# A hybrid attention and retention trunk on one core: the front's hand-written order, decay tables, retention norm and batch 1's x

## The chip, the cores and the metric

The kernel runs on 1 core of one Trainium2 chip. A core has five engines that run beside each other, each with its own instruction stream: TensorE (PE, matmuls; PEld is its weight load), VectorE (DVE), ScalarE (ACT), GpSimd (POOL) and SyncE (SP, which here issues most DMAs). They wait for each other through semaphores. The metric is the device time of one execution in microseconds, the median over runs.

## The reference

Two sequences ("prompt" and "sample", called batch 0 and batch 1 below) of 512 positions with 1024 features pass through one layer, in float32:

```python
mod = silu(c) @ w_ada + b_ada                       # adaLN, six sections of 1024
sh1, sc1, g1, sh2, sc2, g2 = split(mod, 6)
h = rms_norm(x, norm1_g) * (1.0 + sc1) + sh1
proj = h @ w_in                                     # 1024 -> 2816
q_a, k_a, v_a, q_r, k_r, v_r, g_r = split(proj)     # 512, 128, 128, 512, 512, 512, 512
o_a = windowed_attention(q_a, k_a, v_a, sink)       # 8 heads, |t - s| <= 128, ALiBi
o_r = bidirectional_retention(q_r, k_r, v_r, g_r, decay_fwd, decay_bwd)   # 4 heads
x = x + g1 * (concat(o_a, o_r) @ w_out)
h = rms_norm(x, norm2_g) * (1.0 + sc2) + sh2
x = x + g2 * (square(relu(h @ w_mlp1)) @ w_mlp2)    # 1024 -> 4096 -> 1024
return rms_norm(x, final_g)
```

Retention of a head weighs the score of positions t and s by exp(|t - s| * log g), with one decay forward and one backward, and normalizes each row of its result over the head's 128 features: `(y - mean) * rsqrt(var + eps)`, then multiplies by `silu(g_r)`.

## The kernel before

Every product of two matrices is made in three passes of a rounded format: a value is split into a high part (a cast on ACT: `wh`, `hh`) and a low part (value minus high part, on DVE: `wl`, `hl`), and `mm3` (L117) multiplies high by high, high by low and low by high. A weight unit is 128 x 1024 and is loaded, cast and subtracted (`split_unit`, L95) before PE can use it; batch 0 writes both parts back to DRAM (`kept_first`, `kept_rv`, `kept_in`), and batch 1 loads them from there (`kept_unit`, L108).

The program runs in stages. The **front** computes batch 0's RMS norm, the first two adaLN sections for batch 0 and the first six column units of w_in (768 columns: attention's Q, K and V), which are accumulated in six PSUM banks named `first`. Its order is written out by hand in `FRONT` (L1093): a string of steps, issued one after the other, and pinned per engine by `pin` (L1116) up to the first step of P.7. A step's number is a chunk of 128 of the 1024 features (kc, 0 to 7) or a part of it:

- `x`, `nat`, `tr`, `wi` load x, adaLN weights in two layouts, and w_in; `pm`, `mr`, `pt`, `md` make adaLN of a chunk on PE for both batches (from `nat`); `C.kc.1` and `C.kc.0` make it for batch 0 by a reduction on DVE (from `tr`; L170, the tile `jka_f`) for scale and shift.
- `xn` scales x by the norm's factors (L275); `hh` (ACT, L278), `hm` (ACT, L281) and `hl` (DVE, L284) make h's high part, h itself and its low part; `wh` (ACT, L1050) and `wl` (DVE, L1055, the tile `wil`) do the same for w_in.
- `P.kc.c` is one `mm3` of chunk kc and column unit c; 18 matmuls for each kc. `keep.kc` stores both parts of w_in's chunk (`kept_first`) through POOL's DMA queue (L1077). `lg` are the small steps of the decays' logarithms, `cbc` copies of adaLN's input from PSUM.

When P.7 of a column unit is done, its K, V or Q is cast (`ks`, `vt_a`, `qs`: L299 to L329). Then `run_units` goes through the **units** of batch 0: `pj_rv` (retention's V, four units of two), `pj_rq`, `pj_rk`, `pj_rg` of each head, while stages (attention blocks, retention heads), background jobs (adaLN of the other sections, `raw_adat_s` and `raw_adat_g`) and extra jobs are issued between a unit's matmuls. What is issued behind the front is ordered by the framework's scheduler. `norm_x1` (L1118), batch 1's RMS norm, is an extra job that a hook starts behind unit 9. The same units for batch 1 follow, then the output projection and the MLP.

A retention head (`ret_head`, L394) gets its decay table (`decay_table`, L511: an exp over 128 x 896 of distances times logarithms), and at its end takes mean and variance on DVE, the power -1/2 on POOL (`rrs`, L440), and writes four blocks `ryn` (L443) that PE transposes (`pyb`, L448).

Loads of weights go to three buffers (`raw`) or, with `spare`, to a pool of 32 (`r4f`).

## Time and profile before

| | us |
|---|---|
| median of 3 runs | 1139.08 (1136.89 to 1140.65) |
| the profiled execution | 1136.41 |
| its span | 1134.6 |
| mean granted TensorE clock | 0.991 of full speed |
| TensorE busy | 1088.0 |
| VectorE busy | 890.3 |
| ScalarE busy | 488.9 |

In the rows of the profile `A<-B xN` is an instruction that writes tile A from B, N times; a bracket `[3.79 <-DVE h]` is idle time of the engine just ahead of it, in us, with what ended it. `PEclk` is the granted clock of TensorE as a share of full speed. A matmul's own duration (some 0.39 us for 512 columns) is longer than the distance to the next, since matmuls are pipelined.

### The profile page before, as it was taken

How to read it: one execution, taken by the hardware profiler on the slowest of the kernel's cores; microseconds unless marked ns; L12 is line 12 of the kernel's file. 1: busy time of each engine (PE TensorE's matmuls, PEld its weight loads, DVE VectorE, ACT ScalarE, POOL GpSimd, SP SyncE). 2: the span in 40 equal slices, each digit the busy share in tenths (PEclk: the TensorE clock that was granted, in tenths of full speed). 3: DMA queues.
4: the chain of work that ended last, by engine and by line, in shares of the span. 5: the costliest groups of instructions: out<-in, count | busy, mean ns of one | idle time of the engine just before them, and what ended most of it. 6: DMA issues, size and time to landing. Idle time of an engine off the chain costs nothing.

```text
span 1134.6 us, 14030 instructions
## 1 busy us (share of the span) xinstructions
PE 1088.0 (96%) x4997; PEld 888.0 (78%) x4997; DVE 890.3 (78%) x1504; ACT 488.9 (43%) x827; POOL 47.2 (4%) x70
## 2 busy tenths in 40 slices
...
GB/s 374 354 212 247 223 261 322 246 216 195 190 179 162 202 303 338 322 183 23 213 220 158 161 167 177 166 155 130 232 371 103 173 189 194 213 93 185 184 21 148
DMA packets 85722, 232.73 MB, mean 205 GB/s; under 512 B 8578, under 2 KB 20882, under 8 KB 85652
## 3 DMA queue, kind: packets, MB, share of 16 engines
...
q0 software_dynamic: 1440, 6.31, 1.4%
q8 instruction: 39, 0.64, 0.2%
q10 hardware_dynamic: 288, 0.31, 0.1%
...
## 4 chain that ended last, share of the span: by engine, by line
PE 67%; DVE 9%; DMA 2%; issue 2%; ACT 2%; POOL 1%; SPq 0%; POOLq 0%; ACTq 0%; DVEq 0%
PE px_None L898 13%; PE x L1295 13%; PE py_None L898 10%; PE y L1295 10%; PE po L120 2%; PE po L121 2%; PE po L122 2%; PE po L384 1%; PE ppt L377 1%; DVE jka_s L170 1%; DVE wc_l L1235 1%; DVE x2r L1359 1%; DVE jka_g L170 1%; DMA ur<-spill 1%; DMA wl_q<-kept_first 1%
## 5 line engine op out<-in xcount | busy, mean ns | idle before, releaser
L1235 DVE TENSOR_TENSOR uc_l<-ur,uc_h 128x1024 fp32r<-128x1024 f32 x56 | 68.3, 1220 | 53.7 <-ACT uc_h L1235 36.6
L1295 PE MATMUL x<-wc_l,uc_h 128*128 128x512 f32 x256 | 99.8, 390 | 0.8 <-DVE wc_l L1235 0.8
L1295 PE MATMUL x<-wc_h,uc_h 128*128 128x512 f32 x256 | 99.4, 389 | 0.5 <-DVE u L916 0.5
L1295 PE MATMUL x<-wc_h,uc_l 128*128 128x512 f32 x256 | 99.6, 389 | 0.0
L1235 ACT CAST uc_h<-ur 128x1024 fp32r<-128x1024 f32 x56 | 58.9, 1052 | 73.8 <-PE x L1295 30.8
L1295 PE MATMUL y<-wc_h,uc_h 128*128 128x512 f32 x192 | 74.7, 389 | 0.0
L1295 PE MATMUL y<-wc_l,uc_h 128*128 128x512 f32 x192 | 74.7, 389 | 0.0
L1295 PE MATMUL y<-wc_h,uc_l 128*128 128x512 f32 x192 | 74.7, 389 | 0.0
L1235 ACT CAST wc_h<-w 128x1024 fp32r<-128x1024 f32 x48 | 50.4, 1051 | 48.1 <-PE x L1295 23.9
L1235 DVE TENSOR_TENSOR wc_l<-w,wc_h 128x1024 fp32r<-128x1024 f32 x48 | 58.5, 1219 | 13.6 <-ACT wc_h L1235 11.4
L1295 PEld LDWEIGHTS x<-wc_l,uc_h 128*128 128x128 f32 x256 | 48.1, 188 | 11.4 <-DVE wc_l L1235 1.6
L1295 PEld LDWEIGHTS x<-wc_h,uc_h 128*128 128x128 f32 x256 | 48.0, 188 | 10.9 <-issue 0.9
L1295 PEld LDWEIGHTS x<-wc_h,uc_l 128*128 128x128 f32 x256 | 48.1, 188 | 10.0
L120 PE MATMUL po<-wh_wo,ms 128*128 128x512 f32 x128 | 50.2, 396 | 0.0
L122 PE MATMUL po<-wh_wo,ms 128*128 128x512 f32 x128 | 49.6, 390 | 0.0
L121 PE MATMUL po<-wl_wo,ms 128*128 128x512 f32 x128 | 49.5, 389 | 0.0
L361 ACT ACTIVATE st<-st,negm 128x256 f32<-128x256 f32 (+1 forms) x64 | 35.2, 555 | 20.5 <-DVE negm L356 20.5
L803 ACT CAST wc_s4h<-raw_w 128x1024 fp32r<-128x1024 f32 x16 | 16.8, 1053 | 62.2 <-PE px_None L898 41.2
L1295 PEld LDWEIGHTS y<-wc_h,uc_h 128*128 128x128 f32 x192 | 36.0, 188 | 7.5
L1295 PEld LDWEIGHTS y<-wc_h,uc_l 128*128 128x128 f32 x192 | 36.0, 188 | 7.5
L1295 PEld LDWEIGHTS y<-wc_l,uc_h 128*128 128x128 f32 x192 | 36.0, 188 | 7.4
L898 PE MATMUL py_None<-hch,wc_a 128*128 128x512 f32 x120 | 39.7, 390 | 0.1
...
## 6 DMA issues: line engine op xcount, KB each, us to landing
...
raw_ada<-in_w_ada_t_dram SPq DMA_DIRECT2D x12, 512.0 KB, 13.4
...
```

Source lines behind the costliest of these rows:

```text
L120: nc.tensor.matmul(ps, lhs[0], rhs[0], start=start, stop=False)
L121: nc.tensor.matmul(ps, lhs[0], rhs[1], start=False, stop=False)
L122: nc.tensor.matmul(ps, lhs[1], rhs[0], start=False, stop=stop)
L170: nc.vector.tensor_tensor_reduce(junk(f"jka_{name}_{sec}_{kc}_{b}"), t, cb[:, b, :], 1.0, bcol[:, sec * KC + kc:sec * KC + kc + 1] if bias ...
L361: nc.scalar.activation(st[hh][:, :w], st[hh][:, :w], AF.Exp, bias=negm[:, hh:hh + 1], scale=0.125, accum_out=den[:, hh:hh + 1])
L377: nc.tensor.transpose(pt[:, hh * P:(hh + 1) * P], st[hh][:, jj * P:(jj + 1) * P], ident)
L384: nc.tensor.matmul(po, va[:, j0 + jj, g].rearrange("p s e -> p (s e)"), pts[jj][:, s, :], start=(jj == 0 and s == 0), stop=(jj == nj - 1 a ...
L803: nc.scalar.copy(hi, src)
L898: self.last = nc.tensor.matmul(bank[:, cs], x[:, k, :], y, start=first and k == 0 and i == 0, stop=last and k == 3 and i == 2, skip_group_ ...
L1235: last_split[:] = [nc.scalar.copy(hi, src), nc.vector.tensor_sub(lo, src, f(hi))]
L1295: nc.tensor.matmul(out, left[n][x][:, i, ts_], right[n][y][:, i, :], start=first and i == 0 and k == 0, stop=end and i == 1 and k == 2, sk ...
L1359: nc.vector.scalar_tensor_tensor(x, x, r, fin["f", j], ALU.mult, ALU.mult)
```

## The change

Six edits:

1. `keep`'s 16 stores are issued by SP's queue and not by POOL's.
2. `FRONT` is written anew. adaLN on PE now takes chunks 0 and 2 (`BOTH`) in place of 0 and 1, so chunk 1 is reduced on DVE and `first_mods` skips 0 and 2 for batch 1; the four `cbc` copies are all on DVE. The string's tail, old and new, stands in the diff.
3. A decay table is made by an ACT scaling and one DVE step (multiply and minimum) ahead of its exp, in place of three DVE steps.
4. Retention's rows are normalized by four ACT activations with scale `rs` and bias `nb`, which one small DVE step makes, in place of four DVE steps.
5. `norm_x1` starts behind unit 7, issues its four x loads first, yields three times, and yields once more after two squares.
6. adaLN weights of the sections behind the second are loaded into the spare pool.

```diff
+BOTH = (0, 2)
...
     def ada_unit(sec, kc, bs, dst, name, bias=None):
 
-        t = raw_unit(w_ada_t[sec, kc], f"adat_{name}_{sec}_{kc}")
+        t = raw_unit(w_ada_t[sec, kc], f"adat_{name}_{sec}_{kc}", sec > 1)
         reduce_unit(t, sec, kc, bs, dst, name, bias)
...
     def first_mods(b):
 
-        for kc in range(2, KC):
+        for kc in [k for k in range(KC) if k not in BOTH]:
             for s in (1, 0):
...
         rs = small([P, NT], f"rrs_{nm}")
         nc.gpsimd.tensor_tensor(rs, va, neghalf[:, :NT], ALU.pow)
         yn = f2(f"ryn_{nm}")
+        nb = small([P, NT], f"rnb_{nm}")
+        nc.vector.scalar_tensor_tensor(nb, mv[:, :, 0], -1.0, rs, ALU.mult, ALU.mult)
         for t in range(NT):
-            nc.vector.tensor_scalar(yn[:, t * P:(t + 1) * P], pn[:, t * P:(t + 1) * P], mv[:, t, 0:1],
-                                    rs[:, t:t + 1], ALU.subtract, ALU.mult)
+            nc.scalar.activation(yn[:, t * P:(t + 1) * P], pn[:, t * P:(t + 1) * P], AF.Identity, bias=nb[:, t:t + 1],
+                                 scale=rs[:, t:t + 1])
         yield 2
...
-        a2 = r4f(f"dl2_{b}_{h}")[:, :TW]
         dt = mwork.tile([P, TW], F32, tag="dtab", name=f"dtab_{b}_{h}", bufs=2)
-        nc.vector.tensor_scalar(a2, dl, 0.0, nlb[:, h:h + 1], ALU.min, ALU.mult)
-        nc.vector.tensor_scalar(dt, dl, 0.0, lg[:, 0, h:h + 1], ALU.max, ALU.mult)
-        nc.vector.tensor_tensor(dt, dt, a2, ALU.add)
+
+        nc.scalar.activation(dt, dl, AF.Copy, scale=lg[:, 0, h:h + 1])
+        nc.vector.scalar_tensor_tensor(dt, dl, nlb[:, h:h + 1], dt, ALU.mult, ALU.min)
         nc.scalar.activation(dt, dt, AF.Exp)
         nc.sync.dma_start(kept_tables[h], dt)
         return dt
...
     def step_nat(kc, kh):
         t = halves[kc, kh] = r4f(f"raw_ada1_{kc}_{kh}")
-        in_order(nc.sync.dma_start(t, w_ada_first[kc, kh]))
+        in_order(nc.sync.dma_start(t, w_ada_first[BOTH.index(kc), kh]))
...
     def step_keep(kc):
         for s in range(2):
-            nc.gpsimd.dma_start(kept_first[:, kc, s, :], f(wi[kc][s]))
+            nc.sync.dma_start(kept_first[:, kc, s, :], f(wi[kc][s]))
...
-    CB_VECTOR = (0, 1)
+    CB_VECTOR = (0, 1, 2, 3)
...
-xn.3 P.5.2 lg.2 P.5.3 lg.3 wl.6 hh.6 P.5.4 lg.4 hm.6 C.7.1 P.5.5 keep.5 lg.5 hl.6 C.7.0 P.6.0 lg.6
-P.6.1 lg.7 wl.7 hh.7 P.6.2 hm.7 P.6.3 hl.7 P.6.4 P.6.5 keep.6 P.7.0 P.7.1 P.7.2 P.7.3 P.7.4 P.7.5
-keep.7
...
+lg.0 C.7.1 hh.6 P.5.1 lg.1 hm.6 P.5.2 lg.2 C.7.0 P.5.3 lg.3 wl.6 P.5.4 lg.4 hh.7 P.5.5 keep.5 lg.5
+hm.7 hl.6 wl.7 P.6.0 lg.6 P.6.1 lg.7 hl.7 P.6.2 P.6.3 P.6.4 P.6.5 keep.6 P.7.0 P.7.1 P.7.2 P.7.3
+P.7.4 P.7.5 keep.7
...
     def norm_x1():
         v = small([P, NT], "v_x1")
+        xt = [load_x_tile(1, t) for t in range(NT)]
+        yield
+        yield
+        yield
         for t in range(NT):
-            ssq = x_squares(1, t, load_x_tile(1, t))
+            ssq = x_squares(1, t, xt[t])
             nc.vector.tensor_scalar(v[:, t:t + 1], ssq, 1.0 / D, EPS, ALU.mult, ALU.add)
+            if t % 2 == 1:
+                yield
         r = small([P, NT], "r_x1")
         nc.gpsimd.tensor_tensor(r, v, neghalf[:, :NT], ALU.pow)
         xt = [load_x_pair(1, t) for t in range(NT)]
...
-    run_units(units, 1.3, {9: lambda: extra.append(norm_x1())}, pace=1.0)
+    run_units(units, 1.3, {7: lambda: extra.append(norm_x1())}, pace=1.0)
```

SP's instructions at the end of the front's loads, before (`raw_wi` is w_in's last chunk of 768 columns, `raw_rv` are retention V's weight units, `kept_rv` the stores of their parts):

```order
L86 DMA raw_ada_7_0_402<-in_w_ada_t_dram 128x1024
L86 DMA raw_wi_417<-in_w_in_first_dram 128x768
L86 DMA raw_rv_0_604<-in_w_in_v_dram 128x1024
L106 DMA kept_rv_616<-wh_rv_0_606 128x1024
L86 DMA raw_rv_1_610<-in_w_in_v_dram 128x1024
L106 DMA kept_rv_616<-wl_rv_0_607 128x1024
```

and in the changed kernel, from the last four of the 16 stores of w_in's high and low parts (`wih`, `wil`) on:

```order
L1080 DMA kept_first<-wih_429 128x768
L1080 DMA kept_first<-wil_430 128x768
L1080 DMA kept_first<-wih_440 128x768
L1080 DMA kept_first<-wil_441 128x768
L88 DMA raw_rv_0_604<-in_w_in_v_dram 128x1024
L88 DMA raw_rv_1_610<-in_w_in_v_dram 128x1024
L88 DMA raw_adat_s_1_731<-in_w_ada_t_dram 128x1024
L108 DMA kept_rv_616<-wh_rv_0_606 128x1024
L108 DMA kept_rv_616<-wl_rv_0_607 128x1024
L88 DMA raw_rv_2_736<-in_w_in_v_dram 128x1024
```

The stores stood on POOL's queue (its rows 11 to 26) in before; now all 16 stand on SP's between the last load of w_in and the first `raw_rv`, and `raw_rv_1` no longer stands behind a store of `raw_rv_0`'s parts.

ACT's instructions at the end of the front, before, from the cast of w_in's last chunk on (`h_0_6` and `hm_0_6` are chunk 6's high part and h itself, `wh_rv` the high part of retention V's weights):

```order
L1050 CAST wih_445<-raw_wi_417 128x768
L485 ACTIVATE lg_z<-lg_ax 128x8
L91 CAST wh_rv_0_606<-raw_rv_0_604 128x1024
L278 ACTIVATE h_0_6_496<-xt_3_144,mod_s_89,mod_a_87 128x512
L281 ACTIVATE hm_0_6_497<-xt_3_144,mod_s_89,mod_a_87 128x512
L91 CAST wh_rv_1_612<-raw_rv_1_610 128x1024
L278 ACTIVATE h_0_7_531<-xt_3_144,mod_s_89,mod_a_87 128x512
L281 ACTIVATE hm_0_7_532<-xt_3_144,mod_s_89,mod_a_87 128x512
L299 CAST ks_0_553<-first_267 64x512
L300 CAST ks_0_553<-first_267 64x512
L308 COPY vt_a_566<-first_278 128x512
```

and in the changed kernel, from chunk 7's h on:

```order
L283 ACTIVATE hm_0_7_511<-xt_3_144,mod_s_89,mod_a_87 128x512
L522 ACTIVATE dtab_0_1516<-dl,lg 128x896
L522 ACTIVATE dtab_1_1649<-dl,lg 128x896
L524 ACTIVATE dtab_0_1516<-dtab_0_1516 128x896
L301 CAST ks_0_553<-first_264 64x512
L302 CAST ks_0_553<-first_264 64x512
L310 COPY vt_a_566<-first_278 128x512
L524 ACTIVATE dtab_1_1649<-dtab_1_1649 128x896
L301 CAST ks_1_558<-first_264 64x512
L302 CAST ks_1_558<-first_264 64x512
```

and, six further rows of `qs` and `va` on:

```order
L330 CAST qs_1_581<-first_293 64x512
L330 CAST qs_2_589<-first_303 64x512
L93 CAST wh_rv_0_606<-raw_rv_0_604 128x1024
L93 CAST wh_rv_1_612<-raw_rv_1_610 128x1024
L330 CAST qs_3_597<-first_312 64x512
L93 CAST wh_rv_2_738<-raw_rv_2_736 128x1024
L363 ACTIVATE st_0_0_0_643,den_0_0_668<-st_0_0_0_643,negm_0_0_664 128x256
```

Both `wh_rv` casts have moved from among h's chunks 6 and 7 to behind the casts of K, V and Q; the scalings and the exps of two decay tables stand there now. `wh_rv_2` stands right ahead of the first attention exps (`st_0_0_0`) in both.

DVE's instructions around chunk 6's low part, before (`wil` is w_in's low part, `jka_f` adaLN's reduction, `lg_p` steps of the logarithms):

```order
L498 TENSOR_SCALAR lg_p<-lg_w_487 128x8
L500 SCALAR_TENSOR_TENSOR lg_p<-lg_p,lg_w_487 128x8
L1055 TENSOR_TENSOR wil_412<-raw_wi_381,wih_411 128x768
L500 SCALAR_TENSOR_TENSOR lg_p<-lg_p,lg_w_487 128x8 x2
L170 ISA jka_f_7_0_505,mod_a_87<-raw_ada_7_1_390,cb,onep 128x1024
L170 ISA mod_a_87 128x1
L1044 TENSOR_TENSOR mod_a_87<-mod_a_87,cols 128x1
L500 SCALAR_TENSOR_TENSOR lg_p<-lg_p,lg_w_487 128x8 x2
L284 TENSOR_TENSOR h_0_6_496<-hm_0_6_497,h_0_6_496 128x512
L170 ISA jka_f_7_0_516,mod_s_89<-raw_ada_7_0_402,cb,cols 128x1024
L170 ISA mod_s_89 128x1
L500 SCALAR_TENSOR_TENSOR lg_p<-lg_p,lg_w_487 128x8
```

and in the changed kernel:

```order
L498 TENSOR_TENSOR lg_w_494<-lg_w 128x8
L172 ISA jka_f_7_0_496,mod_s_89<-raw_ada_7_0_391,cb,cols 128x1024
L172 ISA mod_s_89 128x1
L502 TENSOR_SCALAR lg_p<-lg_w_494 128x8
L504 SCALAR_TENSOR_TENSOR lg_p<-lg_p,lg_w_494 128x8
L1058 TENSOR_TENSOR wil_430<-raw_wi_404,wih_429 128x768
L504 SCALAR_TENSOR_TENSOR lg_p<-lg_p,lg_w_494 128x8 x4
L286 TENSOR_TENSOR h_0_6_479<-hm_0_6_480,h_0_6_479 128x512
L1058 TENSOR_TENSOR wil_441<-raw_wi_413,wih_440 128x768
```

Chunk 6's `h` stands behind both reductions for chunk 7 now, behind one in before; the subtraction of `wl_rv_0` (row 67 in before, ahead of these) stands at row 100.

ACT's instructions around the squares of batch 1's x (`jk`, `ssq`), before (`pt`, `otmp` belong to attention, `rsc` and `rq` to retention, `wh_rk` and `wh_rg` are weights of the next units):

```order
L288 CAST pt_1_3_1_1564<-ppt_1_3_1_1559 128x512
L91 CAST wh_rk_2_1606<-raw_rk_2_1604 128x1024
L387 COPY otmp_1_3_1587<-po_1_3_1582 64x512
L409 CAST rsc_0_1_1597<-rsf_0_1_1595 128x512
L264 ACTIVATE jk_0_1630,ssq_0_1629<-x_0_1627 128x1024
L264 ACTIVATE jk_1_1636,ssq_1_1635<-x_1_1633 128x1024
L264 ACTIVATE jk_2_1642,ssq_2_1641<-x_2_1639 128x1024
L264 ACTIVATE jk_3_1648,ssq_3_1647<-x_3_1645 128x1024
L521 ACTIVATE dtab_1_1662<-dtab_1_1662 128x896
L409 CAST rsc_1_0_1675<-rsf_1_0_1673 128x512
L288 CAST rq_2_1690<-pj_rq_2_1613 128x512
L409 CAST rsc_0_2_1702<-rsf_0_2_1700 128x512
```

and in the changed kernel:

```order
L290 CAST pt_1_3_1_1571<-ppt_1_3_1_1566 128x512
L266 ACTIVATE jk_0_1590,ssq_0_1589<-x_0_1444 128x1024
L93 CAST wh_rk_2_1621<-raw_rk_2_1619 128x1024
L266 ACTIVATE jk_1_1594,ssq_1_1593<-x_1_1446 128x1024
L389 COPY otmp_1_3_1602<-po_1_3_1597 64x512
L411 CAST rsc_0_1_1612<-rsf_0_1_1610 128x512
L266 ACTIVATE jk_2_1642,ssq_2_1641<-x_2_1448 128x1024
L266 ACTIVATE jk_3_1646,ssq_3_1645<-x_3_1450 128x1024
L411 CAST rsc_1_0_1661<-rsf_1_0_1659 128x512
L290 CAST rq_2_1676<-pj_rq_2_1628 128x512
L93 CAST wh_rg_2_1708<-raw_rg_2_1706 128x1024
L522 ACTIVATE dtab_2_2008<-dl,lg 128x896
```

The four squares stood in one row of four; one other row stands behind the first square now, and two behind the second.

20 lines of the change are left out of this document (10 added, 10 removed).

## The prediction

> **What bounds the kernel now.** I read the busy shares first, then the waits of TensorE (PE), then the stretches in which they lie.
>
> ```profile
> PE 1088.0 (96%) x4997; PEld 888.0 (78%) x4997; DVE 890.3 (78%) x1504; ACT 488.9 (43%) x827; POOL 47.2 (4%) x70
> ...
> PE first L121 <- DVE h L284: 6.4, 4, 3.8
> PE first L120 <- ACT h L278: 3.2, 1, 3.2
> PE pj_q L122 <- DMA wl_q<-kept_first: 2.8, 1, 2.8
> PE rb L271 <- POOL r_x L1125: 2.7, 1, 2.7
> ...
> PE pyb L448 <- DVE ryn L443: 2.1, 2, 1.4
> ...
> PE pj_v L120 <- DMA wh_v<-kept_first: 1.1, 1, 1.1
> ```
>
> PE works for 96% of 1134.6 us and the change takes no matmul of a product away, so only PE's waits and its lower clock are to be had. The largest two, 6.4 and 3.2 us (total, times, longest), are in the front, where batch 0's first projection (`first`) waits for the low and high parts of h. The further waits that the change touches are small: wl_q and wh_v, 2.8 + 1.1 = 3.9 us; rb, 2.7; pyb, 2.1. The front and what lies behind it in stretches of 10 us:
>
> ```profile
> 30.00:40.00 10.00, 8.40 (x36) 6.60 (x36) 8.91 (x13) 4.62 (x6) 1.66 (x4) 1.00 1.02 417
> 50.00:60.00 10.00, 3.18 (x7) 2.19 (x8) 7.83 (x19) 4.26 (x6) 0.54 (x1) 0.66 0.72 265
> 60.00:70.00 10.00, 10.00 (x40) 8.04 (x39) 6.65 (x15) 3.51 (x6) 0.54 (x1) 0.83 0.86 320
> 170.00:180.00 10.00, 5.84 (x18) 3.37 (x17) 7.63 (x14) 5.43 (x10) 1.41 (x1) 0.83 0.94 340
> ```
>
> The columns are the busy times of PE, PEld, DVE, ACT and POOL, then the granted clock, the DMA share and GB/s. At 30 to 40 us the DMA engines are full (1.02, 417 GB/s); at 50 to 60 PE does seven matmuls. The clock falls to 0.66 and 0.83: at half clock that is 6.8 and 3.4 us, together until about 63.4.
>
> ```profile
> 53.03 0.69 PE L120 MATMUL first<-h,wih 128*128 128x512 f32 x1 [3.23 <-ACT h L278]
> 57.51 0.79 PE L121 MATMUL first<-h,wih 128*128 128x512 f32 x1 [3.79 <-DVE h L284]
> ...
> 68.34 0.39 PE L120 MATMUL pj_rv<-wh_rv,h 128*128 128x512 f32 x1
> ...
> 51.22 1.04 ACT L91 CAST wh_rv<-raw_rv 128x1024 fp32r<-128x1024 f32 x1 [1.98 <-DMA raw_rv<-in_w_in_v_dram]
> 52.16 0.81 ACT L278 ACTIVATE h<-xt,mod_s,mod_a 128x512 fp32r<-128x512 f32 x1
> ...
> 55.09 1.28 DVE L170 CUSTOM_DVE_ANT_0 jka_f<-raw_ada,cb,onep 128x1024 bf16<-128x1024 f32 x1
> ...
> 56.77 0.68 DVE L284 TENSOR_TENSOR h<-hm,h 128x512 fp32r<-128x512 f32 x1
> ```
>
> This is P.6, the seventh of eight accumulation steps. Its high part (52.16) stands on ACT behind the cast of wh_rv, a weight of the next stage, whose load lands only then. Its low part (56.77) stands on DVE behind reductions for P.7. Both are late because the loads are. They shared the DMA engines with stores:
>
> ```profile
> q0 software_dynamic: 1440, 6.31, 1.4%
> ...
>   DMA raw_wi<-in_w_in_first_dram: 16.2, 6
> ```
>
> The 6.31 MB on POOL's queue q0 are nearly all the 16 `kept_first` stores (16 x 0.393 MB), and the tile's view of raw_wi says that its casts sat 16.2 us waiting for the loads.
>
> **The front.** With stores behind loads, 20 loads of 512 KB and 8 of 384 KB, 13.6 MB, at 417 GB/s are 32.7 us; from about 5 us the last lands at about 38. ACT is then no longer late: in the new order it has no wh_rv cast before the last hm. What is late next is DVE. Its terms:
>
> ```profile
> 18.99 1.28 DVE L170 CUSTOM_DVE_ANT_0 jka_f<-raw_ada,cb,onep 128x1024 bf16<-128x1024 f32 x1
> ...
> 20.39 0.68 DVE L284 TENSOR_TENSOR h<-hm,h 128x512 fp32r<-128x512 f32 x1
> ...
> 22.98 0.69 DVE L284 TENSOR_TENSOR h<-hm,h 128x512 fp32r<-128x512 f32 x1 [0.39 <-ACT hm L281]
> 23.59 1.22 DVE L275 TENSOR_TENSOR xt<-xt,rb 128x1024 f32<-128x1024 f32 x1
> 24.73 0.95 DVE L1055 TENSOR_TENSOR wil<-raw_wi,wih 128x768 fp32r<-128x768 f32 x1
> 25.60 1.28 DVE L170 CUSTOM_DVE_ANT_0 jka_f<-raw_ada,cb,onep 128x1024 bf16<-128x1024 f32 x1
> 26.80 0.08 DVE L170 DVE_READ_ACCUMULATOR2_ANT mod_a<- 128x1 f32 x1
> ```
>
> From start to next start: a reduction for mod_a with its small steps 1.40 (18.99 to 20.39), one for mod_s 1.20 (as 25.60 to 26.80), hl 0.61, xn 1.14, wil 0.87. I take hl.0 done at 20.4, an estimate: chunk 2 goes to PE in place of chunk 1, so DVE starts P.0 about as it did. From there to the end of hl.6 the new order has 5 x 1.40 + 5 x 1.20 + 6 x 0.87 + 6 x 0.61 + 2 x 1.14 = 24.2, and some 2.4 us of small steps (md, the logs; an estimate from their count, at about as long as READ's row or twice that): 47.0. PE's own pace:
>
> ```profile
> 21.70 0.39 PE L120 MATMUL first<-h,wih 128*128 128x512 f32 x1
> ...
> 28.97 0.39 PE L122 MATMUL first<-h,wil 128*128 128x512 f32 x1
> ```
>
> The nth and (n+32)th matmul, so 0.227 us each: 108 of P.0 to P.5 take 24.5, to about 45.2. So P.6's second pass waits for DVE some 1.6 us, and P.7 ends 35 matmuls later, 47.0 + 7.95 = 54.9, against 68.34 in before (P.7 ran up to pj_rv): **13.4 us earlier**, if DVE waits for nothing; every us of such a wait comes off it.
>
> **What is late behind the front.** In before both wh_rv casts were done by then and pj_rv followed at once. Now they stand behind the casts of K, V and Q:
>
> ```profile
> 66.28 0.58 ACT L299 CAST ks<-first 64x512 fp32r<-64x512 f32 x1 [5.61 <-PE first L122]
> ...
> 68.89 0.58 ACT L299 CAST ks<-first 64x512 fp32r<-64x512 f32 x1 [0.83 <-DVE ks L302]
> ...
> 70.09 2.03 ACT L328 CAST qs<-first 64x512 fp32r<-64x512 f32 x4
> ...
> 72.63 1.55 ACT L328 CAST qs<-first 64x512 fp32r<-64x512 f32 x3
> ```
>
> From the first ks cast to the last of these qs casts ACT took 74.18 - 66.28 = 7.9 us. The new order puts one exp of a decay table (0.95, row below) between the ks, where 0.83 of idle time was: 8.0. First ks at the end of P.7's first unit, 47.0 + 4.0 (P.6) + 0.7 = 51.7; wh_rv's cast at 59.7, done at 60.7 (1.04, row above). Its low part on DVE is of xt's size (1.22), and I add 0.4 for the qs subtractions ahead of it: 62.3. PE has only the small transposes, the first scores and three matmuls to do before, 1.8 us. So it is 68.34 - 62.3 + 1.8 = **7.9 us ahead**, not 13.4.
>
> PE then idles some 5 us in 55 to 61. The idle before 57.51 (3.79) cost the clock up to 63.4, hence (63.4 - 57.5)/2 = 2.9 us. Here between nothing and 3.4; I take 1.3, about half of 2.9. [...]
>
> Front, net: 7.9 - 1.3 = **6.6** (3, with the whole 3.4 of the clock and 1.5 of DVE's waits, to 7.9).
>
> **Batch 1's x.**
>
> ```profile
> 166.09 1.06 ACT L264 ACTIVATE jk<-x 128x1024 bf16<-128x1024 f32 x1 [4.40 <-DMA x<-in_x_dram]
> ...
> 173.18 1.11 PE L271 MATMUL rb<-ident,r_x 128*128 128x128 f32 x4 [2.74 <-POOL r_x L1125]
> 173.95 0.78 PE L120 MATMUL prs<-rq,rk 128*128 128x512 f32 x1
> ```
>
> ACT sat 4.40 us on x's load and everything behind it was late, so PE waited 2.74 for r_x. In the new order the hook fires two units earlier, x loads three steps before use, and other casts stand between the squares. The wait goes (2.7), with the clock of 0.83 in 170 to 180 (3.4 us at half, so 1.7). PE's busy 5.84 of those 10 us leaves 4.16 idle, 1.4 besides the 2.74; I take 1.0 of it: **5.4** (0 to 5.8).
>
> **Kept weights.** The chunks of the later adaLN sections come from the spare pool (r4), so that their loads and wl's on SP's queue stand less behind waits. Of the 3.9 I take **3** (0 to 3.9).
>
> **Retention rows.**
>
> ```profile
> 197.01 1.37 DVE L443 TENSOR_SCALAR ryn<-pyn,mv,rrs 128x128 f32<-128x128 f32 x4 [0.90 <-POOL rrs L440]
> ```
>
> Eight times four steps (1.37) leave DVE; one small step, rnb, stays, and DVE now waits there for POOL's rrs (0.90), with wl casts and rsc behind it. On ACT four ACTIVATE of 128 columns are no row of before: between nothing and 4 x 0.81 (h, 512 columns); I take 1.4, DVE's price. pyb's 2.1 may go: **1**, between -7.2 (the 0.90 at each of eight heads) and 2.1.
>
> **Decay tables.**
>
> ```profile
> L520 DVE TENSOR_TENSOR dtab<-dtab,dl x4: 1076/1084/1093, 153.7 to 230.6; 128x896 f32<-128x896 f32 x4
> ...
> L521 ACT ACTIVATE dtab<-dtab x4: 949/953/961, 154.8 to 231.7; 128x896 f32<-128x896 f32 x4
> ```
>
> DVE keeps one step like L520's (1.08) of three, ACT gets one like L521's (0.95). Both are off PE's path after the front, so nothing; without cover, 4 x 0.95 = 3.8 either way.
>
> **New waits.** wh_rv_2's cast stands on ACT ahead of the first attention exps, as in before, but ACT now reaches it early and waits there for PE's first projection unit; DVE waits at rnb. I charge two casts' length, **-2** (0 to -5).
>
> **The sum.** 6.6 + 5.4 + 3 + 1 - 2 = 14.0 of the profiled run's 1136.41: 1122.4. The median is 2.67 above that run (1139.08): **about 1125**.
>
> **Rivals.**
>
> *Given back.* The 16 stores now stand on SP ahead of raw_rv; the last waits for wil_7, right behind hl.6, done at 47.9.
>
> ```profile
> DMA to landing us min/median/max: 4.6/6.3/7.9
> ```
>
> This is raw_rv's time from issue to landing in before; at its longest it would land at 56, and it must be there by 59.7. If the stores run on past that, or DVE waits in the front, all of the 6.6 goes, and the x and kept loads, 6 us behind 16 stores, return 5 of theirs: 1125 + 11.6 = 1137. For it: DMA was full (1.02). Against: 16 x 0.393 MB at 417 GB/s are 15.1 us, over by 54. [...]
>
> *Slower.* Retention on ACT: the four ACTIVATE wait for rnb, rnb for POOL, and h, hm and wh casts that PE needs stand behind them. Price per head 0.90 + 1.37 = 2.27 if all of it reaches PE, 18.2 for eight: 1125 + 1 + 18.2 = 1144. It makes the kernel slower (by over 0.3%, 3.4 us, about what a measurement here can tell) from (13 + 3.4)/8 = 2.05 a head. For it: DVE waited for rrs at each head. Against: ACT is busy 43%, and PE waited for ryn at two heads only.
>
> *All of it.* No clock loss, no new waits, every wait gone: 7.9 + 5.8 + 3.9 + 2.1 = 19.7: 1119.
>
> **Chances.** Forecast 0.64, all of it 0.12 (both faster), given back 0.14 (within 0.3%), slower 0.10. So faster 0.76, same 0.14, slower 0.10. Range: the terms' low ends reach past 1135, so it goes to 1138 with most of the given-back case, and down to 1114 for all of it with the front's whole 13.4 (5.5 more, if PE finds work ready in the idle stretch); outside are the slower case and tails.
>
> **What would show it.** Right: stores in the DMA view after the loads, P.6's wait for h under 2 us, P.7 done near 55, PE's next wait 4 to 6 us, for wh_rv or wl_rv, rb's wait gone, ryn on ACT with no pyb wait. Wrong: `first` still waiting over 3 us for h; a wait for raw_rv's load; pyb's or rsc's waits over 1 us at most heads; the clock below 1 in 60 to 70.

## The result, and the profile after

| | before | changed |
|---|---|---|
| median, us | 1136.62 (1133.85 to 1140.65, 6 runs) | 1144.22 (1143.61 to 1146.14, 6 runs) |
| ratio to before | | 1.0067 (95% interval 1.0044 to 1.009) |
| the profiled execution, its span | 1136.41, 1134.6 | 1146.14, 1144.4 |
| mean granted clock | 0.991 | 0.986 |

The kernel became slower by 0.67%, some 7.6 us; 1125 had been forecast, with a range of 1114 to 1138, and the result lies outside it. The page of the changed kernel, its first line of busy times and POOL's DMA queue:

```profile
PE 1095.9 (96%) x4997; PEld 893.3 (78%) x4997; DVE 878.1 (77%) x1474; ACT 502.3 (44%) x861; POOL 40.8 (4%) x54
...
q0 software_dynamic: 160, 0.02, 0.0%
```

PE has as many instructions as before and is busy for 7.9 us more; since the matmuls are the same, that is a lower clock (0.986 against 0.991). The 6.31 MB have left q0. What PE waited for (total, times, longest):

```profile
PE pyb L452 <- ACT ryn L447: 6.5, 5, 4.2
PE py L122 <- ACT rsc L411: 4.9, 5, 2.1
PE psc L353 <- DVE qs L331: 4.3, 2, 2.2
PE pyn L433 <- ACT ryt L429: 3.0, 1, 3.0
PE pj_rq L122 <- DVE rv L291: 2.8, 1, 2.8
...
PE first L123 <- DVE h L286: 1.4, 2, 1.1
```

The waits of before are nearly gone: `first` waits 1.4 us in place of 9.6, the wait of rb for batch 1's x (2.7) and those for wl_q and wh_v are no longer in the list. Others are new: pyb 6.5, py 4.9, pyn, pj_rq. The stretches that the prediction named, and then three longer ones that cover batch 1 up to the output projection (busy PE, PEld, DVE, ACT, POOL, then granted clock, DMA share, GB/s):

```profile
50.00:60.00 10.00, 7.21 (x34) 5.65 (x32) 7.16 (x10) 9.60 (x16) 0.00 (x0) 1.00 0.90 338
60.00:70.00 10.00, 8.46 (x26) 6.69 (x27) 8.96 (x18) 3.41 (x5) 0.00 (x0) 0.66 0.65 219
170.00:180.00 10.00, 9.39 (x43) 7.15 (x42) 8.52 (x17) 6.50 (x9) 0.00 (x0) 1.00 0.88 318
...
210.00:310.00 100.00, 90.15 (x415) 71.27 (x414) 72.33 (x184) 41.26 (x102) 2.73 (x3) 0.97 0.57 183
310.00:385.00 75.00, 73.52 (x347) 60.02 (x346) 56.27 (x138) 29.30 (x67) 0.86 (x1) 1.00 0.54 178
385.00:415.00 30.00, 20.51 (x70) 14.28 (x69) 20.69 (x41) 10.35 (x21) 1.15 (x2) 0.77 0.50 183
```

In the front and at 170 to 180 PE does more (7 matmuls became 34 in 50 to 60; 18 became 43 in 170 to 180, at full clock), though the clock is 0.66 in 60 to 70. The loss is behind them: in 385 to 415 PE is idle for 9.5 of 30 us and works at a clock of 0.77 for the rest. Starts of PE's work show the same, in us:

| start of | before | changed |
|---|---|---|
| first pj_rv of batch 0 | 68.34 | 62.11 |
| first pj_q of batch 1 | 229.21 | 213.52 |
| last pj_q of batch 1 | 263.46 | 250.00 |
| last pj_rv of batch 1 | 297.62 | 285.68 |
| last pj_rg of batch 1 | 396.03 | 390.35 |
| first matmul of the output projection (po) | 400.26 | 407.14 |
| end of PE | 1125.89 | 1135.62 |

The changed kernel is 15.7 us ahead at the first pj_q, more than the sum of 14 that was forecast, 5.7 ahead at the last pj_rg and 6.9 behind at the output projection. From there to the end little is added.

Two places make the loss. **The first is at 250 to 300.** SP's DMA issues there (start, length of the issue; an issue that waits is long):

```profile
250.56 0.42 SPq L88 DMA_DIRECT2D raw_adat_s<-in_w_ada_t_dram  x1
251.08 14.16 SPq L117 DMA_DIRECT2D wl_rv<-kept_rv  x2
265.34 0.38 SPq L117 DMA_DIRECT2D wh_rq<-kept_in  x1
265.77 0.42 SPq L88 DMA_DIRECT2D raw_adat_s<-in_w_ada_t_dram  x1
```

Two loads of wl_rv stood at the head of SP's queue for 14.16 us, and the next adaLN load stood behind them until 265.77. What SP waited for in 200 to 310 says why:

```profile
SPq L117 <- PE pj_rv L124: 30.7, 4, 13.6
SPq L117 <- PE pj_q L124: 23.8, 4, 8.8
```

L117 is the load of a kept part; it waits for PE to be done with a buffer of split weights. Before, it was released in this stretch by something else too:

```profile
SPq L115 <- DVE gm L170: 15.8, 5, 4.7
```

There a kept load also waited for a DVE reduction, since adaLN's loads and wl's shared the three `raw` buffers: each took its turn. With edit 6, wl's loads have these three to themselves, run ahead, and then stand at SP's head until PE frees a buffer: in these 110 us the kept loads waited some 85 us for PE, against 40 before. DVE comes to the reduction before its data are there and stands idle for 4.33 us, and two waits of PE follow:

```profile
273.13 1.29 DVE L172 CUSTOM_DVE_ANT_0 jka_s<-raw_adat_s,cb,onep 128x1024 bf16<-128x1024 f32 x1 [4.33 <-DMA raw_adat_s<-in_w_ada_t_dram]
```

```profile
276.56 1.71 PE L379 MATMUL ppt<-ident,st 128*128 128x128 f32 x12 [1.67 <-ACT st L371]
...
289.56 0.63 PE L122 MATMUL pj_rq<-h,wh_rq 128*128 128x512 f32 x1 [2.79 <-DVE rv L291]
```

Over the whole run DVE waited as follows (before: jka_s 9.6 in 6 waits, longest 2.4, and no wait for raw_adat_g):

```profile
DVE jka_s L172 <- DMA raw_adat_s<-in_w_ada_t_dram: 12.3, 6, 4.3
DVE jka_g L172 <- DMA raw_adat_g<-in_w_ada_t_dram: 11.4, 5, 3.5
DVE rnb L445 <- POOL rrs L442: 8.8, 8, 1.2
```

**The second is at 391 to 407.** DVE's timeline, at the last but one retention head's statistics (`bn`, of the transposed result `pyn`):

```profile
391.69 1.28 DVE L172 CUSTOM_DVE_ANT_0 jka_s<-raw_adat_s,cb,cols 128x1024 bf16<-128x1024 f32 x1
...
395.30 1.28 DVE L172 CUSTOM_DVE_ANT_0 jka_s<-raw_adat_s,cb,cols 128x1024 bf16<-128x1024 f32 x1
...
396.51 0.29 DVE L437 BATCH_NORM_STATS2 bn<-pyn 128x6 f32<-128x128 f32 x1
```

Between them are two more: four reductions in a row, 4.8 us, and only then the statistics. ACT and PE at the same time:

```profile
393.06 0.59 ACT L429 COPY ryt<-py 128x512 f32<-128x512 f32 x1 [3.75 <-DVE mod_s L172]
399.47 1.50 ACT L447 ACTIVATE ryn<-pyn,rnb,rrs 128x128 f32<-128x128 f32 x4 [5.82 <-DVE rnb L445]
```

```profile
393.70 0.66 PE L433 MATMUL pyn<-ident,ryt 128*128 128x128 f32 x4 [2.97 <-ACT ryt L429]
...
399.98 1.52 PE L452 MATMUL pyb<-ident,ryn 128*128 128x128 f32 x4 [4.23 <-ACT ryn L447]
...
406.55 0.80 PE L122 MATMUL py<-rsc,rv 128*128 128x512 f32 x1 [2.09 <-ACT rsc L411]
```

The copy `ryt` waits for the first of these reductions, because a reduction's discarded output and `ryt` take buffers of the same small pool (f2); `ryn` waits for the statistics behind the fourth. PE's three waits are 9.3 us, and the four transposes pyb take 1.52 here, against 0.66 for pyn six us earlier: the granted clock is 0.50 in 400 to 410. So the list of waits names ACT (pyb for ryn, 6.5), but what ends last in this trace is DVE's row of reductions.

### The profile page after: what moved, and what is told of

It is laid out like the page before. It is cut to its first block, busy times and chain, and to the rows that moved or that the text cites. A ratio compares the mean times of both kernels' runs of the same rounds, so it can differ in the third digit from the quotient of the medians.

```text
span 1144.4 us, 14016 instructions
## 1 busy us (share of the span) xinstructions
PE 1095.9 (96%) x4997; PEld 893.3 (78%) x4997; DVE 878.1 (77%) x1474; ACT 502.3 (44%) x861; POOL 40.8 (4%) x54
## 4 chain that ended last, share of the span: by engine, by line
PE 68%; DVE 16%; DMA 8%; ACT 3%; issue 3%; POOL 1%; SPq 1%; POOLq 0%; DVEq 0%; ACTq 0%
PE px_None L901 12%; PE x L1304 11%; PE y L1304 10%; PE py_None L901 9%; PE po L122 3%; PE po L123 2%; PE po L124 2%; DVE jka_s L172 2%; DMA raw_adat_s<-in_w_ada_t_dram 2%; DMA raw_adat_g<-in_w_ada_t_dram 2%; PE ppt L379 1%; PE po L386 1%; PE psc L353 1%; DMA ur<-spill 1%; DVE jka_f L172 1%
## 5 line engine op out<-in xcount | busy, mean ns | idle before, releaser
L1244 DVE TENSOR_TENSOR wc_l<-w,wc_h 128x1024 fp32r<-128x1024 f32 x48 | 58.5, 1220 | 13.6 <-ACT wc_h L1244 11.4
L122 PE MATMUL po<-wh_wo,ms 128*128 128x512 f32 x128 | 51.8, 405 | 0.0
L124 PE MATMUL po<-wh_wo,ms 128*128 128x512 f32 x128 | 50.9, 398 | 0.0
L806 ACT CAST wc_s4h<-raw_w 128x1024 fp32r<-128x1024 f32 x16 | 16.8, 1052 | 62.2 <-PE px_None L901 36.6
L363 ACT ACTIVATE st<-st,negm 128x256 f32<-128x256 f32 (+1 forms) x64 | 35.2, 555 | 15.5 <-DVE negm L358 15.5
L411 ACT CAST rsc<-rsf 128x512 fp32r<-128x512 f32 x32 | 19.7, 621 | 49.2 <-DVE rsf L409 49.2
```

The costliest lines, as they stand in the source:

```text
L122: nc.tensor.matmul(ps, lhs[0], rhs[0], start=start, stop=False)
L124: nc.tensor.matmul(ps, lhs[1], rhs[0], start=False, stop=stop)
L363: nc.scalar.activation(st[hh][:, :w], st[hh][:, :w], AF.Exp, bias=negm[:, hh:hh + 1], scale=0.125, accum_out=den[:, hh:hh + 1])
L411: nc.scalar.copy(sc[sb][:, 0, :], sf)
L806: nc.scalar.copy(hi, src)
L1244: last_split[:] = [nc.scalar.copy(hi, src), nc.vector.tensor_sub(lo, src, f(hi))]
```

## The experiments

Medians in us; ratios to the kernel before, run beside it, with their 95% intervals. Sections of adaLN are counted from 0, as in the code: 2 is the first gate (`jka_g`), 3 the second shift, 4 the second scale (both `jka_s`). Several expectations call section 3 the third, and 2 and 4 the second and fourth; it is this count.

### Which edit costs

Edit 6 undone, and edit 6 alone on the kernel before:

```diff
-        t = raw_unit(w_ada_t[sec, kc], f"adat_{name}_{sec}_{kc}", sec > 1)
+        t = raw_unit(w_ada_t[sec, kc], f"adat_{name}_{sec}_{kc}")
```

> The changed kernel with edit 6 alone undone: adaLN weights of the sections behind the second come from the three raw buffers again. Theory A (edit 6 is the loss: these loads now stand on SP's queue behind kept loads that wait for PE, and DVE waits for them in its order): raw_adat_g's wait on DVE falls from 11.4 us to under 3, the four reductions in a row ahead of head 1's statistics at 391.7 to 396.5 split up, about 13 of the 17 us of lead at 250 us survive, about 1128 us (1124 to 1133). Theory B (edit 4, retention's normalization on ACT, is the loss): 1142 to 1146, as the changed kernel. Theory C (PE that is ahead meets loads that can't come earlier, whatever pool they use): 1137 to 1144, with the loads' waits under other names.

> The kernel before with edit 6 alone. Theory A: raw_adat_g's wait on DVE appears here too (over 5 us), 1140 to 1150. Theory B: as before, 1134 to 1139. Theory C: as before, since PE is not ahead here, 1134 to 1139.

Without edit 6: 1114.2 (1112.16 to 1114.98), 0.9788 (0.9771 to 0.9806). Edit 6 alone: 1160.43, 1.0203 (1.0183 to 1.0222). So edit 6 costs 30.0 us on top of the other five, and 23.2 alone, and the other five gain 23. Theory A named the right edit and put it too low: no6 came out 10 us under its range and only6 10 above. The changed kernel without it, in the same three stretches, and what DVE waited for:

```profile
210.00:310.00 100.00, 98.37 (x484) 80.83 (x483) 85.00 (x223) 49.30 (x122) 2.74 (x3) 1.00 0.64 207
310.00:385.00 75.00, 74.86 (x348) 61.26 (x348) 61.30 (x136) 30.67 (x67) 2.01 (x2) 1.00 0.58 197
385.00:415.00 30.00, 30.00 (x137) 24.83 (x137) 18.63 (x34) 13.19 (x24) 1.01 (x1) 1.00 0.87 307
```

```profile
DVE jka_s L172 <- DMA raw_adat_s<-in_w_ada_t_dram: 1.6, 4, 0.7
DVE jka_g L172 <- DMA raw_adat_g<-in_w_ada_t_dram: 1.5, 2, 1.1
```

PE is busy 98.37 of 100 us where it was 90.15, and 30.00 of 30 where it was 20.51, at full clock. The waits for adaLN's loads fell from 23.7 to 3.1: the larger pool made these loads later, not earlier (the eight of raw_adat_g are issued from 173.3 to 244.9 us in the changed kernel, from 165.0 to 230.4 without edit 6).

Retention's rows back on DVE (and `rnb` left out), with edit 6 and without:

```diff
-            nc.scalar.activation(yn[:, t * P:(t + 1) * P], pn[:, t * P:(t + 1) * P], AF.Identity, bias=nb[:, t:t + 1],
-                                 scale=rs[:, t:t + 1])
+            nc.vector.tensor_scalar(yn[:, t * P:(t + 1) * P], pn[:, t * P:(t + 1) * P], mv[:, t, 0:1],
+                                    rs[:, t:t + 1], ALU.subtract, ALU.mult)
```

> The changed kernel with edit 4 alone undone: retention's rows are normalized by four DVE steps again. Theory A: 1141 to 1147, waits for raw_adat_g and jka_s stay. Theory B: 1128 to 1133, and pyb's waits (6.5 us) go. Theory C: 1140 to 1146.

> Edits 1, 2, 3 and 5 (no6 with retention's normalization on DVE again). By the term on record (edit 4 worth 1 us): 1115. By no4 against the changed kernel (5 us): 1119. By the rival on record that ACT pays up to 2.3 us a head: 1096 to 1110.

With edit 6 the kernel got slower by undoing edit 4, and slower than any of the three theories said: 1149.59, 1.0102 (1.0085 to 1.0119), so edit 4 is worth 4 (by the ratios) to 5.4 (by the medians) there, with intervals that just overlap. Without edit 6 it is 1115.09, 0.98 (0.9779 to 0.9821), against 0.9788: edit 4 is worth 0.9 by the medians, less than the intervals tell apart. The rival in which ACT's rows make the kernel slower is out, although pyb's wait for them heads PE's list.

Edits 1 and 2 alone on the kernel before (the edits 3 to 6 undone):

> Edits 1 and 2 alone (the new front with the stores on SP); decay tables, retention norm, batch 1's x and the pools as before. Theory A: the front's lead survives, 1128 to 1133. Theory B: 1128 to 1133 too. Theory C: 1135 to 1141: the lead is gone by 400 us.

1127.3 (1125.94 to 1132.11), 0.9917 (0.9892 to 0.9943): the front gains 9.9 by the medians. Its profiled execution was its slowest, 1132.11, 4.3 faster than the profiled one of before.

### Where edit 6 costs

The same loads into the same spare pool, issued by POOL's queue (`raw_unit` takes the queue as one more argument):

```diff
-        t = raw_unit(w_ada_t[sec, kc], f"adat_{name}_{sec}_{kc}", sec > 1)
+        t = raw_unit(w_ada_t[sec, kc], f"adat_{name}_{sec}_{kc}", sec > 1, nc.gpsimd if sec > 1 else None)
```

> The changed kernel with edit 6, but these adaLN loads issued by POOL's queue and not SP's. Theory A1 (the loss is SP's order: the loads stand behind kept loads that wait for PE to free a weight buffer, and DVE waits for them): the wait for raw_adat_g on DVE falls from 11.4 us to under 4 and most of the 30 us comes back, 1114 to 1126 us. Theory A2 (the loss is DVE's order: the reductions are put early and in a row because their buffers are free, whoever issues the loads): 1136 to 1146, with the row of four reductions ahead of head 1's statistics still there.

1133.44, 0.9962 (0.9946 to 0.9977): 10.8 faster than the changed kernel. DVE's wait for raw_adat_g is gone and that for raw_adat_s is 2.3, and the last pj_rv starts at 275.34 in place of 285.68. The last pj_rg starts at 377.90; it is at 390.35 in the changed kernel and at 376.40 in no6, so 12.45 of the 13.95 us lost up to there are back. The place at 250 to 300 was SP's order, then. The other 19.2 us against no6 remain, and the time lies between the ranges of the two theories: A1 holds for the first place alone. On POOL's queue, too, loads stood behind a wait: POOL's timeline, and the first of the four reductions on DVE.

```profile
371.45 1.03 POOL L442 TENSOR_TENSOR rrs<-rva,neghalf 128x4 f32<-128x4 f32 x1 [23.29 <-DVE rva L440]
372.45 1.11 POOL L88 DMA_DIRECT2D raw_adat_s<-in_w_ada_t_dram  x2
```

```profile
378.82 1.28 DVE L172 CUSTOM_DVE_ANT_0 jka_s<-raw_adat_s,cb,cols 128x1024 bf16<-128x1024 f32 x1 [1.45 <-DMA raw_adat_s<-in_w_ada_t_dram]
```

Two loads stood behind a retention head's power (`rrs`), which waited 23.29 us; the four reductions then ran at 378.82 to 383.65, ahead of the statistics, and PE waited 2.5 for ryt, 5.0 for ryn, 3.1 for rsc.

The spare pool for section 3 only (`sec == 3`), and for sections 2 and 4 only (`sec in (2, 4)`):

```diff
-        t = raw_unit(w_ada_t[sec, kc], f"adat_{name}_{sec}_{kc}", sec > 1)
+        t = raw_unit(w_ada_t[sec, kc], f"adat_{name}_{sec}_{kc}", sec == 3)
```

> no6 with the spare pool for one adaLN section only, the third (its reductions, jka_s with cols, run beside batch 1's last retention heads). The order on DVE has the four reductions in a row ahead of head 1's statistics again, as in the changed kernel. Theory A2 (that row costs what is lost at 385 to 405 in the changed kernel, also with nothing else late): 12 to 16 us, 1126 to 1131, with PE's waits for ryt and ryn there and no wait for raw_adat_g over 2 us. Theory A1 alone (only loads behind kept loads matter): 1113 to 1117.

> no6 with the spare pool for the second and fourth adaLN sections only (the counterpart of sec3_spare; their reductions run at 180 to 330 us). If the two parts add up to edit 6's 30 us: 1114.2 + (1144.2 - 1129.7) = about 1129 (1125 to 1132), with raw_adat_g's waits on DVE (over 8 us) and the lead lost between 220 and 310 us, and nothing lost at 370 to 405. If the third section's loads make the others late too: under 1121. If the losses overlap: over 1135.

1129.72, 0.9933 (0.9907 to 0.9959), and 1133.15 (1129.16 to 1135.64, 9 runs), 0.9953 (0.9933 to 0.9972): against no6's 1114.2 section 3 costs 15.5 and the two others 19.0, 34.5 in sum against the 30.0 of all three. PE's busy time and granted clock in the three stretches tell them apart:

| | 210 to 310 | 310 to 385 | 385 to 415 | whole run, us |
|---|---|---|---|---|
| before | 93.09, 1.00 | 74.58, 1.00 | 28.75, 1.00 | 1137 |
| changed | 90.15, 0.97 | 73.52, 1.00 | 20.51, 0.77 | 1144.2 |
| edit 6 alone | 85.02, 0.94 | 74.68, 0.99 | 25.97, 0.94 | 1160.4 |
| changed, loads on POOL | 96.25, 0.98 | 69.85, 0.98 | 23.61, 0.82 | 1133.4 |
| changed, sections 2 and 4 only | 89.90, 0.97 | 73.16, 1.00 | 29.88, 1.00 | 1133.2 |
| changed, section 3 only | 98.39, 1.00 | 68.75, 0.99 | 26.27, 0.91 | 1129.7 |
| changed without edit 6 | 98.37, 1.00 | 74.86, 1.00 | 30.00, 1.00 | 1114.2 |

Sections 2 and 4 make the whole loss at 210 to 310, section 3 nearly all of that at 310 to 415. PE's starts say the same: from the last pj_rg to the first matmul of the output projection it is 2.4 us in no6 and with sections 2 and 4 only, 10.7 with section 3 only, 16.8 in the changed kernel and 18.4 with the loads on POOL. Section 3's four reductions stand in one row ahead of the statistics in the changed kernel, in that with the loads on POOL and in that with section 3 alone; in no6 two of them stand ahead of the scores `rsc` that come before. With section 3 alone the immediate waits are others than in the changed kernel: ACT's copy stands behind a cast that waits for its load, and DVE waits 14.3 us for raw_adat_s in the whole run, against 1.6 in no6.

```profile
376.69 1.04 ACT L93 CAST wh_wo<-raw_wo 128x1024 fp32r<-128x1024 f32 x1 [4.57 <-DMA raw_wo<-in_w_out_dram]
377.64 0.58 ACT L429 COPY ryt<-py 128x512 f32<-128x512 f32 x1
```

So that the place is section 3's is shown; which share of it is the row, which the shared buffer of `ryt` and which the loads, is not. A buffer of its own for the reductions' discarded output wasn't tried.

### The other edits, on top of no6

One more edit undone each, with edit 6 undone in all three. The decay tables' one DVE step back to three (with its buffer `a2`):

```diff
-        nc.scalar.activation(dt, dl, AF.Copy, scale=lg[:, 0, h:h + 1])
-        nc.vector.scalar_tensor_tensor(dt, dl, nlb[:, h:h + 1], dt, ALU.mult, ALU.min)
+        nc.vector.tensor_scalar(a2, dl, 0.0, nlb[:, h:h + 1], ALU.min, ALU.mult)
+        nc.vector.tensor_scalar(dt, dl, 0.0, lg[:, 0, h:h + 1], ALU.max, ALU.mult)
+        nc.vector.tensor_tensor(dt, dt, a2, ALU.add)
```

> Edits 1, 2, 4 and 5 (no6 with the decay tables in three DVE steps). By the difference of front_only (1127.3), no46 (1115.1) and edit 5's share (2.9): edit 3 is worth about 9, 1121 to 1125. By the term on record (nothing): 1113 to 1116.

1124.08, 0.9883 (0.986 to 0.9907): the tables are worth 9.9, the largest of these edits, where nothing was forecast. From 70 to 170 us PE is as busy as in no6, within 0.1 us in each 10. Then PE waits where no6 does not:

```profile
173.22 0.50 PE L123 MATMUL py<-rsc,rv 128*128 128x512 f32 x1 [2.23 <-DVE rsc L412]
175.70 0.66 PE L433 MATMUL pyn<-ident,ryt 128*128 128x128 f32 x4 [1.04 <-ACT ryt L429]
```

In 170 to 180 PE is busy 6.56 in place of 9.47 and DVE all of the 10 us, against 8.80. In DVE's order just ahead of these scores:

```profile
169.61 1.23 DVE L277 TENSOR_TENSOR xt<-xt,rb 128x1024 f32<-128x1024 f32 x1 [1.05 <-DMA xt<-in_x_t_dram]
170.75 0.68 DVE L523 TENSOR_SCALAR dtab<-dl,lg 128x896 f32<-128x896 f32 x1
...
172.49 1.29 DVE L412 TENSOR_TENSOR rsc<-rsf,rsc 128x512 fp32r<-128x512 f32 x2
```

DVE comes to them at 172.49, in no6 at 166.38. One table step stands there, and two more (0.68 and 1.09) at 159 to 161; scalings of batch 1's x, a wait for its load and a reduction stand there too, in another order than in no6. A table's three steps take 2.45 us of DVE against 1.15 for the one, so 5.2 us for four tables; how they become 9.9 of the whole isn't shown.

Batch 1's x with its loads and squares in one row, from unit 9 on:

```diff
-    run_units(units, 1.3, {7: lambda: extra.append(norm_x1())}, pace=1.0)
+    run_units(units, 1.3, {9: lambda: extra.append(norm_x1())}, pace=1.0)
...
-            ssq = x_squares(1, t, xt[t])
+            ssq = x_squares(1, t, load_x_tile(1, t))
```

> Edits 1, 2, 3 and 4 (no6 with batch 1's x as before). By the term on record (5.4 us): 1119 to 1121, with PE's wait for r_x of about 2 us and a half clock behind it. If the wait only moves elsewhere: 1114 to 1116.

1117.12, 0.9818 (0.9799 to 0.9837): 2.9 by the medians, between the two expectations. rb's wait is 0.67 there, and a longer one for wh_rq stands behind it, whose cast ACT reaches at 175.74, behind four activations of batch 1's h (no6: at 171.32):

```profile
176.83 0.50 PE L122 MATMUL pj_rq<-h,wh_rq 128*128 128x512 f32 x1 [3.07 <-ACT wh_rq L93]
```

The front's stores on POOL's queue:

```diff
-            nc.sync.dma_start(kept_first[:, kc, s, :], f(wi[kc][s]))
+            nc.gpsimd.dma_start(kept_first[:, kc, s, :], f(wi[kc][s]))
```

> Edits 2, 3, 4 and 5 (no6 with the 16 stores on POOL's queue again, where they start as soon as their data is there). If the order of stores and loads is what the front gains by: first waits over 3 us for h again, 1118 to 1126. If the new step order alone is: 1113 to 1116.

1117.16, 0.9821 (0.9797 to 0.9845): 3.0 by the medians, between what was expected if the stores' order were the whole gain of the front and if it were none of it. In the new order with the stores on POOL, P.6's waits return:

```profile
49.84 0.50 PE L122 MATMUL first<-h,wih 128*128 128x512 f32 x1 [1.69 <-ACT h L280]
...
54.97 0.79 PE L123 MATMUL first<-h,wih 128*128 128x512 f32 x1 [4.62 <-DVE h L286]
```

P.7's last matmul starts 9.0 us later than in no6 (64.92, 55.88), but the first pj_rv only 3.0 (65.1, 62.1).

For both the intervals overlap no6's a little; the waits in the traces are what carries them.

### Towards a better version

no6 still idles behind the front, since retention V's weights are cast only behind K, V and Q. Here they are loaded among the front's stores and split at its end:

```diff
-C.6.0 P.4.1 wh.7 P.4.2 wl.5 P.4.3 hl.5 P.4.4 xn.3 P.4.5 keep.0 keep.1 keep.2 keep.3 keep.4 P.5.0
+C.6.0 P.4.1 wh.7 P.4.2 wl.5 P.4.3 hl.5 P.4.4 xn.3 P.4.5 keep.0 keep.1 keep.2 keep.3 keep.4 rvl.0 P.5.0
...
-hm.7 hl.6 wl.7 P.6.0 lg.6 P.6.1 lg.7 hl.7 P.6.2 P.6.3 P.6.4 P.6.5 keep.6 P.7.0 P.7.1 P.7.2 P.7.3
+hm.7 hl.6 wl.7 P.6.0 lg.6 P.6.1 lg.7 hl.7 rvs.0 P.6.2 P.6.3 P.6.4 P.6.5 keep.6 rvs.1 P.7.0 P.7.1 P.7.2 P.7.3
```

(`rvl.1` stands behind `keep.5`; `rvl` loads a unit, `rvs` casts and subtracts it.)

> no6 with retention V's first two weight units loaded among the front's stores (rv_0 ahead of chunk 5's, rv_1 ahead of chunk 6's) and split at the front's end. If the idle time behind P.7 is the wait for wh_rv and wl_rv: PE's waits for psc at 56 and 59 us (4.3 us) shrink to under 1, the clock stays at 1 in 60 to 70, 1106 to 1110 us. If PE is held there by the casts of Q and by PSUM banks instead: 1112 to 1115.

The first pj_rv starts at 56.08 in place of 62.12, the waits for psc are gone, and there is no idle time and no lower clock behind it:

```profile
60.00:70.00 10.00, 10.00 (x50) 8.40 (x49) 9.86 (x23) 5.31 (x11) 0.00 (x0) 1.00 0.72 272
```

Yet the time is 1114.19, 0.9791 (0.977 to 0.9812), that of no6: the 6 us are gone by 140 us, among them a wait of 1.83 for wl_rg. Batch 0's first units ran ahead, but their loads share the three raw buffers with the adaLN sections 0 and 1. So these two got the spare pool (`sec < 2`), and then all of their chunks but the last two (`sec < 2 and kc < 6`):

```diff
-        t = raw_unit(w_ada_t[sec, kc], f"adat_{name}_{sec}_{kc}", sec > 1)
+        t = raw_unit(w_ada_t[sec, kc], f"adat_{name}_{sec}_{kc}", sec < 2 and kc < 6)
```

> early_rv with the spare pool for the first two adaLN sections of batch 1 only (loads beside batch 0's units, where no kept loads stand on SP). early_rv was 6.3 us ahead of no6 at 67 us and level at 140. If the three raw buffers take that lead (weight loads behind reductions): the lead at 150 us stays over 3, 1107 to 1111. If DVE's work takes it (8.2 of 10 us busy): 1112 to 1116.

> early_rv with the spare pool for batch 1's first two sections in chunks 1, 3, 4 and 5 only; the spare loads of chunks 6 and 7 were late at 160 to 175 us in early_rv_spare01, which was 7 us ahead of no6 at 150. If those two chunks' loads were its loss: 1106 to 1112. If the loss comes with any spare load: 1114 to 1124.

With all chunks 1123.14, 0.988 (0.9856 to 0.9904), slower than either expectation: the lead held past 140 us (PE is busy for all of 60 to 140), so the shared buffers were what had taken it. Then loads came late: DVE waited 3.58 for raw_adat_s at 173.96, ACT 5.72 for the load of raw_rg at 175.24, and PE behind both:

```profile
176.86 0.49 PE L122 MATMUL py<-rsc,rv 128*128 128x512 f32 x1 [3.07 <-ACT rsc L411]
```

Without chunks 6 and 7 it is **1111.28** (1110.78 to 1112.1), 0.9763 (0.9746 to 0.978), the fastest run of this study; its interval still overlaps no6's.

## Why the prediction was wrong

**The step that failed is "Kept weights".** It put edit 6 at a gain of 3 (0 to 3.9), "so that their loads and wl's on SP's queue stand less behind waits". Measured, it is a loss of 30.0. The range was bounded by the waits that could go (wl_q and wh_v) and had no lower end below nothing, though nothing excluded a loss. What the step missed: sharing three buffers was also what made the two kinds of loads take turns. Freed from it, wl's loads ran ahead to the head of SP's queue and waited there for PE (14.16 us at 251), with adaLN's loads behind them; and reductions were bunched in DVE's order ahead of a retention head's statistics (four in a row, 4.8 us). The first was shown by moving the loads to another queue (12.45 us earlier at the last pj_rg), the place of the second by section 3 alone; which share of the second is DVE's row stays open. The forecast without this step, 1125 + 3 = 1128, would still have been 14 above no6's 1114.2.

**Decay tables** were put at nothing, since they were "off PE's path after the front". They are worth 9.9 (no36): the mis-sized term on the other side. The cover that was assumed did not exist at 170 to 180, where DVE with the three steps was busy for all of the 10 us; and the price named for no cover, 3.8, is well under 9.9 too.

**The front.** P.6's wait was forecast at 1.6 and is 1.1; pj_rv was forecast at 62.3 and came at 62.11. That it agrees so well is partly luck: 62.3 was the end of wl_rv's subtraction, which came at 63.97, and wh_rv's cast began at 60.86 and not 59.7; but the first matmuls of pj_rv need wh_rv alone. PE's next wait was put at 4 to 6 us, for wh_rv or wl_rv; it is 4.34 in two parts, and names qs. That idle time and the clock behind it:

```profile
48.01 0.50 PE L123 MATMUL first<-h,wih 128*128 128x512 f32 x1 [1.10 <-DVE h L286]
...
58.92 0.50 PE L353 MATMUL psc<-ks,qs 128*128 128x256 f32 x2 [2.22 <-DVE qs L331]
61.54 0.77 PE L353 MATMUL psc<-ks,qs 128*128 128x256 f32 x2 [2.12 <-DVE qs L331]
62.11 1.07 PE L122 MATMUL pj_rv<-wh_rv,h 128*128 128x512 f32 x2
```

The clock was put at 1.3, the author's choice between nothing and 3.4 (about half of a 2.9 worked out from before's rows); no run shows the 1.3. At 0.66 in 60 to 70 it is 3.4, the upper end: in steps of 1 us the granted clock of the changed kernel is 0.50 from 62 to 67. In before it was 0.58 in 53 to 54 and 0.50 from 54 to 63, so it was low already ahead of most of the 3.79 us of idle time to which the prediction put it. So the front's net in the trace is 7.9 - 3.4 = 4.5, not 6.6, and the work done on PE at 72 to 120 us is some 4 to 5.5 us ahead of before (an estimate, by the matmul columns in the traces of before, the changed kernel, no6 and front_only). By the medians of edits 1 and 2 alone it is 9.9, with an interval (6.5 to 12.3, from the ratios) that does not hold 4.5; that kernel's own profiled execution gives 4.3. Which of the two holds is open. The stores, which the prediction put first, are worth 3.0 of it (no16); the rest lies in edit 2, whose parts weren't run apart.

**Batch 1's x** was put at 5.4 and is 2.9: rb's wait went, as forecast, but in the new front without edit 5 it would only have been 0.67, and the rest of the term was a wait for wh_rq.

**Retention rows** were put at 1 and are 0.9 without edit 6, not told from nothing. rnb waited for rrs at each of eight heads (8.8 in all, 1.1 each, against the 0.90 assumed), and it hardly reached PE: 1.7 us of pyb's waits in no6. The slower rival had the steps' length about right (0.90 + 1.37 a head, measured 1.1 + 1.50), but hardly any of it reached PE; that its time, 1144, is the measured one is luck, since the loss came from another edit.

**Given back** did not happen in the front. The stores ended in time (the last was issued at 50.57, and wh_rv's cast at 60.86 waited for no load), and PE waited for no load of raw_rv.

**New waits** (2) were not measured by themselves.

The sum of single gains without edit 6, 9.9 for edits 1 and 2 (on the kernel before), then 9.9, 0.9 and 2.9 (undone from no6), is 23.6, against the 23 measured together.
